# Wider weight operations, two-bank PSUM tiles and five more seven-product pairs in a hybrid encoder block

## The chip, the cores and the metric

The kernel runs on one core of one Trainium2 chip. The metric is the device time of one execution in microseconds (us); lower is better. The engines are named as in the profile: PE is the matrix engine (TensorE) and PEld its weight loads, DVE is VectorE, ACT is ScalarE, POOL is GpSimd, SP issues most of the loads. Work moves between HBM, the on-chip SBUF, and PSUM, the eight banks (128 partitions x 512 floats each) in which matmuls accumulate.

## The reference

One layer over 256 tokens of width 2048, all in float32:

```python
hn = rmsnorm(h, mix_norm_pre)
z, xbc, dt_raw, u = jnp.split(hn @ w_in, ...)             # 2048 x 3616
y_ssd = ssd_mixer(z, xbc, dt_raw, ...)                    # bidirectional Mamba-2 scan, 16 heads of 64
y_pool = pool_mixer(u, pool_w, pool_scale)                # centred mean pooling, 4 windows
h = h + rmsnorm(concat([y_ssd, y_pool]) @ w_out, mix_norm_post)      # 2048 x 2048
hn = rmsnorm(h, ffn_norm_pre)
gate, val = jnp.split(hn @ w_ffn_up, 2, axis=-1)          # 2048 x 11264
ff = (gelu(dwconv(gate, ffn_conv_w, ffn_conv_b)) * val) @ w_ffn_down # 5632 x 2048
h = h + rmsnorm(ff, ffn_norm_post)
gate = sigmoid(rmsnorm(h, ple_norm_pre) @ w_ple_gate)     # 2048 x 2048
h = h + rmsnorm(gate * (p @ w_ple), ple_norm_post)
```

Every weight is used for 256 tokens only, so each is loaded from HBM once, prepared once and used by a few matmuls.

## The kernel before

**Split weights.** The matmuls run on float32r operands. For more precision each float32 weight block is split into a high part (ACT casts it, line 153) and a low part (DVE subtracts the high part from the raw weights, line 154). A product is then three matmuls: high x high, high x low, low x high. The raw weights land in a buffer with tag `raw` (128 x 2048 floats, three of them, line 158); the halves go into tiles with tags `whi` and `wlo` (1056 columns, five of each, lines 149 and 150). One load of 2048 columns, called a unit here, is split as two parts of 1024. A buffer is given again when its last reader has finished, and the tile framework puts in the waits.

**Stages, in order of time.** The first projection `dtu` (dt and the pooling input), three slabs of the conv projection `xbc`, the `z` projection, the output projection `wo`, a small per-layer embedding product `ple`, the up-projection (`ga` and `va`, 176 pieces of 1024 weight columns, line 1010), the down-projection `dn`, and the embedding gate `gt`. `wo`, `dn` and `gt` are done in two halves of 1024 output columns; a half is a loop over pairs of row blocks (`token_major`, line 305). A pair is two 128-row blocks of the weights against two 128-token blocks and two 512-column blocks.

**Pairs by seven products.** A pair is normally 8 block products, 24 matmuls of 512 columns. For pairs listed in `fast`, `dn_fast` and `gt_fast`, `seven_products` (line 255) uses a Strassen-like scheme with 7 products, 21 matmuls. It needs sums of weight blocks (`add_blocks`, line 249: four in-place adds of 512 columns) and sums of activation blocks (`pair_sums`, line 784). For most pairs of `dn` and `gt` the sums of the weight blocks are made during the up-projection (`block_sums`, line 226: fetch, add, store to HBM through POOL's queue) and loaded again as `t`; the pair then loads 1536 raw columns as `r` and 2048 of sums as `t`. Where no sums were made, the pair does its adds in the raw buffer, in place: split part of it, add, split the result. Parts are split as four tiles: `a` (512), `b`, `d`, `c` (1024 each). Activation sums of `dn` are made early for the pairs in `dn_stored`, kept in HBM as `hsum` and fetched as `hd`.

**Order.** In the up-projection ACT, DVE and SP follow the order of the program (`in_order`, line 199); everywhere else the framework's scheduler orders each engine's queue. In the up-projection the parts are split five pieces ahead of their matmuls (line 1008), so the split of part n + 5 waits for piece n. The loads stand on SP's queue in the program's order, each waiting for a free raw buffer; the fetches of the block sums stand between them.

**PSUM.** Two pools: `pmain`, six banks handed out one at a time (`main` takes two), and `pmisc`, two banks. `total` (line 367) adds the two 256-column halves of a bank with one ACT copy and one DVE add per bank.

Of the kernel before, what the change touches and what calls it, by code (L numbers as in the profile page):

```python
# [53 lines left out]
def build(nc, a, out):  # L54
# [6 lines left out]
    with tile.TileContext(nc) as tc, \  # L61
# [6 lines left out]
            tc.tile_pool(name="pmain", bufs=6, space=bass.MemoryType.PSUM) as pm, \  # L68
# [14 lines left out]
        def main(name):  # L83
            return [pm.tile([P, 512], F32, tag="main", name=f"{name}_{i}") for i in range(2)]
# [14 lines left out]
        r0 = wp.tile([P, 2048], F32, tag="raw", bufs=3, name="dtur0")  # L99
# [42 lines left out]
        def split(name, src, nel, cuts=()):  # L142

            if name in ready:
                return ready.pop(name)
            if name in spare:
                hi, lo = spare.pop(name)
            else:
                hi = wp.tile([P, 1056], F32R, tag="whi", bufs=5, name=f"{name}h")
                lo = wp.tile([P, 1056], F32R, tag="wlo", bufs=5, name=f"{name}l")  # L150
            for c0, c1 in zip((0, *cuts), (*cuts, nel)):
                s = slice(c0, c1)
                last["act"] = ins(nc.scalar.copy(hi[:, s], src[:, s]))
                last["dve"] = ins(nc.vector.tensor_sub(lo[:, s], src[:, s], hi[:, s].bitcast(F32)))
            return hi, lo

        def raw(name, src=None):
            r = wp.tile([P, 2048], F32, tag="raw", bufs=3, name=name)
            if src is not None:
                last["dma"] = load(r, src, True)  # L160
            return r

# [86 lines left out]
        def add_blocks(r):  # L249

            v = r.rearrange("p (b c) -> p b c", b=4)
            for i, j in ((1, 0), (0, 3), (3, 1), (2, 3)):
                nc.vector.tensor_add(v[:, i], v[:, i], v[:, j])  # L253

        def seven_products(name, stage, w, k0, c0, a_, acc, alt, start, stop):

            if (stage, c0, k0) in sums_:
                r = raw(f"{name}r")  # L260
                last["dma"] = load(r[:, 512:], w[c0 // 1024, k0 // 2][:, 512:], True)
                t, held = sums_[stage, c0, k0]
                if not held:
                    t = page(f"{name}t")
                    last["dma"] = load(t, sums_[stage, c0, k0][0], True)
            else:
                r = t = raw(f"{name}r", w[c0 // 1024, k0 // 2])
            b11 = split(f"{name}a", r[:, 512:1024], 512)
            b2 = split(f"{name}b", r[:, 1024:], 1024)
            if r is t:  # L270
                add_blocks(r)
            t42 = split(f"{name}d", t[:, 1024:], 1024)
            t31 = split(f"{name}c", t[:, :1024], 1024)

            for x, (wh, wl), c, o, own in (
                    ("a11", b11, 0, alt[0], True), ("a12", b2, 0, acc[0][0], False), ("a22", t42, 0, acc[1][0], False),
                    ("s4", b2, 512, acc[0][1], False), ("s2", t42, 512, alt[3], True), ("s1", t31, 512, alt[1], True),
                    ("s3", t31, 0, alt[2], True)):
                xh, xl = a_[x]
                for q, (xx, ww) in enumerate(((xh, wh), (xh, wl), (xl, wh))):  # L280
                    mm(o, xx, ww[:, c:c + 512], own and start and q == 0, own and stop and q == 2)
# [23 lines left out]
        def token_major(name, w, c0, ks, get, acc, tail=1, fast=(), alt=None, sums=None, at=()):  # L305
# [3 lines left out]
            for u in range(nu):  # L309
# [8 lines left out]
                r = None if f"{name}{k0}_0" in ready else raw(f"{name}r{k0}", w[c0 // 1024, k0 // 2])  # L318
                for j in range(2):
                    group.append((k0 + j, *split(f"{name}{k0}_{j}", r and r[:, j * 1024:(j + 1) * 1024], 1024)))  # L320
# [18 lines left out]
        def feature_major(name, w, get, acc):  # L339

            for u in range(4):
                r = raw(f"{name}r{u}", w[u])
                for j in range(2):
                    wh, wl = split(f"{name}{u}_{j}", r[:, j * 1024:(j + 1) * 1024], 1024)
                    for kk in range(2):
                        k = 4 * u + 2 * j + kk
                        xh, xl = get(k)
                        for f in range(4):
                            s = slice(kk * 512 + f * P, kk * 512 + (f + 1) * P)
                            for q, (ww, xx) in enumerate(((wh, xh), (wh, xl), (wl, xh))):  # L350
                                mm(acc[f // 2][:, f % 2 * L:(f % 2 + 1) * L], ww[:, s], xx,
                                   k == 0 and q == 0 and f % 2 == 0, k == NK - 1 and q == 2)
                aside()

        def feature_pairs(n, part, get, acc):

            wh, wl = part
            for kk in range(4):  # L360
                k = 4 * n + kk
                for f in range(2):
                    s = slice(kk * 256 + f * P, kk * 256 + (f + 1) * P)
                    mm(acc[f], wh[:, s], get.both(k), k == 0, False)
                    mm(acc[f][:, L:], wl[:, s], get(k)[0], False, k == NK - 1)

        def total(o, acc):

            for f in range(2):
                nc.scalar.copy(o[:, f * L:(f + 1) * L], acc[f][:, L:])  # L370
                nc.vector.tensor_add(o[:, f * L:(f + 1) * L], o[:, f * L:(f + 1) * L], acc[f][:, :L])
# [82 lines left out]
        for u in range(0, NK, 2):  # L454
            r = [wp.tile([P, 2048], F32, tag="raw", bufs=3, name=f"dtur{u}") if u else r0, page(f"dtur{u + 1}")]
# [19 lines left out]
            for j in range(2):  # L475
                k = u + j
                with tc.issue_after(front[0]), tc.issue_after(front[1]):
                    wh, wl = split(f"dtu{k}", r[j][:, :1056], 1056, ((352, 704), (704,))[k] if k < 2 else ())
# [305 lines left out]
        def pair_sums(name, s, o, a11, a21, a12, a22):  # L784


            s1, s2, s3, s4 = (s[:, i * P:(i + 1) * P] for i in range(4))
            nc.vector.tensor_sub(s1, a22, a21)
            nc.vector.tensor_sub(s3, a11, a21)
# [6 lines left out]
        def sums_in(o):  # L796
            return {f"s{i + 1}": (o[:, i * P:(i + 1) * P], o[:, 512 + i * P:512 + (i + 1) * P]) for i in range(4)}

        class Sums:
# [5 lines left out]
            def __call__(self, k):  # L805
                if k not in self.got:
                    n = len(self.got)
                    if n % 2 == 0:
# [6 lines left out]
                                            *(v[:, i * P:(i + 1) * P] for i in range(4)))  # L815
# [53 lines left out]
        for t in range(2):  # L869
            load(h[t], x[t * P:(t + 1) * P, :])  # L870
        hf = sublayer("wo", w_out, list(range(8, 16)) + list(range(8)), cat, gload("gmix", a["mix_norm_post"][0]), h,
                      V_FN, Pairs, ((5,), (2, 4)), Sums("cs", cat))
# [26 lines left out]
        for t in range(2):  # L899
# [3 lines left out]
        dn_fast, gt_fast = ((2, 3, 4, 5, 7, 8, 9, 10, 11, 12, 13, 14, 15, 16, 17, 18, 19), (2, 3, 4, 5, 7, 8, 9, 11, 12, 13, 14, 15, 16, 18, 19)), ((4, 5, 6), (1, 2))  # L903

        dn_stored = (2, 3, 5, 7, 8, 10, 11, 13, 14, 16, 17, 18, 19)
        gt_ks = list(range(NK)), [0, 1, 8, 9, 10, 11, 2, 3, 4, 5, 6, 7, 12, 13, 14, 15]
        which = [("dn", w_down, c * 1024, 2 * u) for c in range(2) for u in dn_fast[c]] + \
            [("gt", w_gate, c * 1024, gt_ks[c][2 * u]) for c in range(2) for u in gt_fast[c]]
# [26 lines left out]
        def hid_sums_of(k, s, o):  # L935
            return pair_sums(f"he{k}", s, o, *(hid_part(k)[:, i * P:(i + 1) * P] for i in range(4)))
# [24 lines left out]
        def next_part():  # L961

            n = len(parts)
            if n < NPIECES:
                s, v, i = blocks[n // 4]
                name = f"u{'gv'[v]}{s}{i}"
                if n % 2 == 0:
                    slab["raw"] = raw(f"{name}r{n // 2 % 2}", w_up[v, s, i, n // 2 % 2])
                parts.append(split(f"{name}{n // 2 % 2}_{n % 2}", slab["raw"][:, n % 2 * 1024:(n % 2 + 1) * 1024], 1024))
# [37 lines left out]
        with in_order():  # L1007
            for _ in range(5):
                next_part()
            for n in range(NPIECES):  # L1010
                s, v, i = blocks[n // 4]
                if n % 4 == 0:
                    acc = main(f"{'gv'[v]}a{s}{i}")
# [9 lines left out]
                next_part()  # L1023
# [38 lines left out]
        def ple_parts():  # L1062

            r = raw("ple1r0", w_ple[1, 0])
            for j in range(2):
                ready[f"ple10_{j}"] = split(f"ple10_{j}", r[:, j * 1024:(j + 1) * 1024], 1024)
# [7 lines left out]
        def first():  # L1074

            r, hi, lo = page("gtf"), page("gtfh", F32R), page("gtfl", F32R)
            last["dma"] = load(r, w_gate[0, 0])
            for j in range(2):
                c = slice(j * 1024, (j + 1) * 1024)
                spare[f"gt00_{j}"] = hi[:, c], lo[:, c]  # L1080
                ready[f"gt00_{j}"] = split(f"gt00_{j}", r[:, c], 1024)
# [49 lines left out]
        for half in range(2):  # L1131
# [5 lines left out]
            if half == 1:  # L1137

                for i in (8, 10):
                    sh, sl = page(f"gth{i}", F32R), page(f"gtl{i}", F32R)  # L1140
                    for j in range(2):
                        spare[f"gt1{ks[i]}_{j}"] = (sh[:, j * 1024:(j + 1) * 1024], sl[:, j * 1024:(j + 1) * 1024])
# [99 lines left out]
```

## Time and profile before

| | |
|---|---|
| time, median of three runs | 1116.89 us (1116.58 to 1117.33) |
| span of the profiled execution | 1115.6 us |
| the profiled execution's own time | its span is what the profile gives; the median of the runs is 1.3 us above it |
| PE busy | 1104.8 us, 99% |
| PEld, DVE, ACT, POOL busy | 951.8, 957.5, 721.7, 68.5 us |
| moved by transfers | 347.29 MB, 311 GB/s on average |
| up-projection, about 304 to 788 us | PE without a gap, transfers at 372 GB/s |
| down-projection, about 788 to 1009 us | PE 215.66 of 216 us busy from 790 to 1006 |

How to read it: a page shows one execution. Busy shares are followed by the span in 40 equal slices, each digit the busy tenths of an engine in that slice. The chain of work that ended last is followed back from the last instruction. A timeline row gives start, duration, engine, line, operation, output and inputs; a group row gives count, total busy us and mean ns of one. A waits row says which engine and line waited for which, in total us, times, and the longest. A transfers row gives count, size of one and the median us from issue to landing. The matmuls' ends are modelled, so the pace of PE is read from the distance of starts.

### The profile page before, as it was taken

How to read it: one execution, taken by the hardware profiler on the slowest of the kernel's cores; microseconds unless marked ns; L12 is line 12 of the kernel's file. 1: busy time of each engine (PE TensorE's matmuls, PEld its weight loads, DVE VectorE, ACT ScalarE, POOL GpSimd, SP SyncE). 2: the span in 40 equal slices, each digit the busy share in tenths (PEclk: the TensorE clock that was granted, in tenths of full speed). 3: DMA queues.
4: the chain of work that ended last, by engine and by line, in shares of the span. 5: the costliest groups of instructions: out<-in, count | busy, mean ns of one | idle time of the engine just before them, and what ended most of it. 6: DMA issues, size and time to landing. Idle time of an engine off the chain costs nothing.

```text
span 1115.6 us, 16022 instructions
## 1 busy us (share of the span) xinstructions
PE 1104.8 (99%) x5948; PEld 951.8 (85%) x5948; DVE 957.5 (86%) x1334; ACT 721.7 (65%) x1048; POOL 68.5 (6%) x140
## 2 busy tenths in 40 slices
PE   9999999999999999999999999999999999999997
PEld 9999988888888888888888888888888888877876
DVE  6478997799868898888888888888899999989895
ACT  6847662555775564665655645657589778867673
POOL 0200000100100000000000000000000000001001
PEclk9999999999999999999999999999999999999999
DMA  9752447454599999999899999999999899996763
GB/s 362 314 194 109 164 156 284 151 189 158 199 362 401 387 378 376 359 375 369 346 377 382 354 380 366 353 391 391 361 379 382 329 343 400 418 376 229 264 237 105
DMA packets 54943, 347.29 MB, mean 311 GB/s; under 512 B 6096, under 2 KB 6992, under 8 KB 20176
## 3 DMA queue, kind: packets, MB, share of 16 engines
q1 hardware_dynamic: 44064, 289.53, 67.3%
q0 software_dynamic: 10368, 56.10, 13.4%
q8 instruction: 47, 0.77, 0.3%
q10 hardware_dynamic: 432, 0.62, 0.2%
q14 instruction: 32, 0.26, 0.1%
HBM read 297.48 MB, written 48.76 MB: 310 GB/s over the span
## 4 chain that ended last, share of the span: by engine, by line
PE 94%; DVE 2%; ACT 1%; DMA 1%; issue 1%; POOL 0%; POOLq 0%; ACTq 0%; DVEq 0%
PE ga L90 22%; PE va L90 22%; PE dna L90 12%; PE woa L90 7%; PE xbc L90 5%; PE gt L90 5%; PE z L90 4%; PE dns L90 4%; PE dtu L90 4%; PE dn0s L90 2%; PE dn1s L90 2%; DMA dtur<-w_dtu 1%; PE pw L90 1%; PE yd L90 1%; PE gts L90 1%
## 5 line engine op out<-in xcount | busy, mean ns | idle before, releaser
L90 PE MATMUL ga<-wox,ug_0h 128*128 128x512 f32 x352 | 125.5, 395 | 0.0
L90 PE MATMUL ga<-wox,ug_1h 128*128 128x512 f32 x352 | 125.1, 394 | 0.0
L90 PE MATMUL va<-wox,uv_1h 128*128 128x512 f32 x352 | 124.8, 393 | 0.0
L90 PE MATMUL va<-wox,uv_0h 128*128 128x512 f32 x352 | 124.8, 393 | 0.0
L90 PE MATMUL ga<-wox,ug_1l 128*128 128x256 f32 x352 | 99.1, 282 | 0.0
L90 PE MATMUL va<-wox,uv_1l 128*128 128x256 f32 x352 | 99.1, 281 | 0.0
L90 PE MATMUL va<-wox,uv_0l 128*128 128x256 f32 x352 | 99.1, 281 | 0.0
L90 PE MATMUL ga<-wox,ug_0l 128*128 128x256 f32 x352 | 99.0, 281 | 0.0
L253 DVE TENSOR_TENSOR dnb<-dnb 128x512 f32<-128x512 f32 x128 | 88.3, 690 | 3.1
L90 PEld LDWEIGHTS va<-wox,uv_1h 128*128 128x128 f32 x352 | 66.1, 188 | 15.0
L90 PEld LDWEIGHTS va<-wox,uv_0h 128*128 128x128 f32 x352 | 66.1, 188 | 15.0
L90 PEld LDWEIGHTS ga<-wox,ug_1h 128*128 128x128 f32 x352 | 66.1, 188 | 15.0
L90 PEld LDWEIGHTS ga<-wox,ug_0h 128*128 128x128 f32 x352 | 66.1, 188 | 14.8
L90 PEld LDWEIGHTS ga<-wox,ug_0l 128*128 128x128 f32 x352 | 66.2, 188 | 0.1
L90 PEld LDWEIGHTS ga<-wox,ug_1l 128*128 128x128 f32 x352 | 66.2, 188 | 0.0
L90 PEld LDWEIGHTS va<-wox,uv_1l 128*128 128x128 f32 x352 | 66.2, 188 | 0.0
L90 PEld LDWEIGHTS va<-wox,uv_0l 128*128 128x128 f32 x352 | 66.2, 188 | 0.0
L928 ACT CAST hs<-hid 128x512 fp32r<-128x512 f32 x44 | 27.3, 621 | 21.9 <-PE dna L90 21.6
L244 POOL DMA_DIRECT2D dns<-dnb x30 | 16.3, 542 | 309.4 <-DVE dnb L253 309.4
L929 DVE TENSOR_TENSOR hs<-hid,hs 128x512 fp32r<-128x512 f32 x44 | 30.1, 685 | 5.9 <-ACT hs L928 5.9
L792 ACT CAST he<-he 128x512 fp32r<-128x512 f32 x13 | 8.1, 621 | 36.6 <-DVE he L791 36.6
L90 PE MATMUL dna<-dn_1h,hs 128*128 128x512 f32 x96 | 30.9, 393 | 0.0
(2242 smaller groups left out, 3214.8 us busy)
## 6 DMA issues: line engine op xcount, KB each, us to landing
dnb<-w_down SPq DMA_DIRECT2D x32, 1024.0 KB, 9.9
dns<-dnb POOLq DMA_DIRECT2D x30, 1024.0 KB, 6.9
hd<-hsum POOLq DMA_DIRECT2D x24, 512.0 KB, 8.3
zr<-w_z SPq DMA_DIRECT2D x8, 1024.0 KB, 4.8
dtur<-w_dtu SPq DMA_DIRECT2D x14, 528.0 KB, 8.9
wo0r<-w_out_ SPq DMA_DIRECT2D x7, 1024.0 KB, 4.8
dn1r<-w_down SPq DMA_DIRECT2D x7, 1024.0 KB, 6.6
hsum<-he POOLq DMA_DIRECT2D x13, 512.0 KB, 7.9
```

Source lines behind the costliest of these rows:

```text
L90: last["pe"] = ins(nc.tensor.matmul(o, lhsT, rhs, start=start, stop=stop, skip_group_check=True))
L244: nc.gpsimd.dma_start(t, pg[0])
L253: nc.vector.tensor_add(v[:, i], v[:, i], v[:, j])
L792: nc.scalar.copy(o[:, :512], s[:, :512])
L928: nc.scalar.copy(t[:, :512], hid_part(k))
L929: nc.vector.tensor_sub(t[:, 512:], hid_part(k), t[:, :512].bitcast(F32))
```

## The change

Weight parts are made in one operation of 2048 columns (1536 and 2048 in a pair by seven products) where there were two to four smaller ones. `whi` and `wlo` become three tiles of 2112 columns each in place of five of 1056; the raw buffers become two in place of three. A pair of PSUM banks becomes one tile of 1024 columns, with three tiles in the pool, and `total` handles both banks in one operation per engine. `add_blocks` does its first two adds in one operation with a reversed access pattern; `pair_sums` does two of its subtractions in one.

Five more pairs use seven products, all made in place: pair 6 in the first half of `dn`, pairs 6 and 10 in its second half, pair 5 in the second half of `wo`, pair 3 in the first half of `gt`. In `dn` the in-place pairs use a page instead of a raw buffer. The list of sums made early is the same as before; one more set of activation sums (of pair 6) is stored, and three more are fetched. In the first projection two of the loads that used raw buffers change to other tiles (one is a page).

```diff
-            tc.tile_pool(name="pmain", bufs=6, space=bass.MemoryType.PSUM) as pm, \
+            tc.tile_pool(name="pmain", bufs=3, space=bass.MemoryType.PSUM) as pm, \
...
         def main(name):
-            return [pm.tile([P, 512], F32, tag="main", name=f"{name}_{i}") for i in range(2)]
+            o = both_banks(name)
+            return [o[:, :512], o[:, 512:]]
+
+        def both_banks(name):
+            return pm.tile([P, 1024], F32, tag="main", name=name)
...
-        def split(name, src, nel, cuts=()):
-
-            if name in ready:
-                return ready.pop(name)
-            if name in spare:
-                hi, lo = spare.pop(name)
-            else:
-                hi = wp.tile([P, 1056], F32R, tag="whi", bufs=5, name=f"{name}h")
-                lo = wp.tile([P, 1056], F32R, tag="wlo", bufs=5, name=f"{name}l")
+        def halves(name):
+            return tuple(wp.tile([P, 2112], F32R, tag=f"w{q}", bufs=3, name=f"{name}{q}") for q in ("hi", "lo"))
+
+        def split(hi, lo, src, nel, cuts=()):
+
             for c0, c1 in zip((0, *cuts), (*cuts, nel)):
                 s = slice(c0, c1)
                 last["act"] = ins(nc.scalar.copy(hi[:, s], src[:, s]))
                 last["dve"] = ins(nc.vector.tensor_sub(lo[:, s], src[:, s], hi[:, s].bitcast(F32)))
-            return hi, lo
+            return hi[:, :nel], lo[:, :nel]
 
         def raw(name, src=None):
-            r = wp.tile([P, 2048], F32, tag="raw", bufs=3, name=name)
+            r = wp.tile([P, 2048], F32, tag="raw", bufs=2, name=name)
...
+        def unit(name, src):
+
+            if name in ready:
+                return ready.pop(name)
+            r = raw(f"{name}r", src)
+            return split(*(spare.pop(name) if name in spare else halves(name)), r, 2048)
...
             v = r.rearrange("p (b c) -> p b c", b=4)
-            for i, j in ((1, 0), (0, 3), (3, 1), (2, 3)):
+            nc.vector.tensor_add(v[:, 1::-1], v[:, 1::-1], v[:, ::3])
+            for i, j in ((3, 1), (2, 3)):
                 nc.vector.tensor_add(v[:, i], v[:, i], v[:, j])
...
             else:
-                r = t = raw(f"{name}r", w[c0 // 1024, k0 // 2])
-            b11 = split(f"{name}a", r[:, 512:1024], 512)
-            b2 = split(f"{name}b", r[:, 1024:], 1024)
+                r = t = page(f"{name}r") if stage == "dn" else raw(f"{name}r")
+                last["dma"] = load(r, w[c0 // 1024, k0 // 2], True)
+            bh, bl = split(*halves(f"{name}b"), r[:, 512:], 1536)
             if r is t:
                 add_blocks(r)
-            t42 = split(f"{name}d", t[:, 1024:], 1024)
-            t31 = split(f"{name}c", t[:, :1024], 1024)
+            th, tl = split(*halves(f"{name}t"), t, 2048)
+            b11, b2, t31, t42 = ((h_[:, c0:c1], l_[:, c0:c1]) for h_, l_, c0, c1 in
+                                 ((bh, bl, 0, 512), (bh, bl, 512, 1536), (th, tl, 0, 1024), (th, tl, 1024, 2048)))
...
-            for f in range(2):
-                nc.scalar.copy(o[:, f * L:(f + 1) * L], acc[f][:, L:])
-                nc.vector.tensor_add(o[:, f * L:(f + 1) * L], o[:, f * L:(f + 1) * L], acc[f][:, :L])
+            o, a_ = (v.rearrange("p (f t) -> p f t", f=2) for v in (o, acc))
+            nc.scalar.copy(o, a_[:, :, L:])
+            nc.vector.tensor_add(o, o, a_[:, :, :L])
...
-            r = [wp.tile([P, 2048], F32, tag="raw", bufs=3, name=f"dtur{u}") if u else r0, page(f"dtur{u + 1}")]
+            r = [r0 if u == 0 else page(f"dtur{u}") if u == 4 else raw(f"dtur{u}"), page(f"dtur{u + 1}")]
+            pair = halves(f"dtu{u}")
...
-                      V_FN, Pairs, ((5,), (2, 4)), Sums("cs", cat))
+                      V_FN, Pairs, ((5,), (2, 4, 5)), Sums("cs", cat))
...
-        dn_fast, gt_fast = ((2, 3, 4, 5, 7, 8, 9, 10, 11, 12, 13, 14, 15, 16, 17, 18, 19), (2, 3, 4, 5, 7, 8, 9, 11, 12, 13, 14, 15, 16, 18, 19)), ((4, 5, 6), (1, 2))
-
-        dn_stored = (2, 3, 5, 7, 8, 10, 11, 13, 14, 16, 17, 18, 19)
+        dn_fast, gt_fast = (tuple(range(2, 20)), tuple(u for u in range(2, 20) if u != 17)), ((3, 4, 5, 6), (1, 2))
+
+        dn_stored = (2, 3, 5, 6, 7, 8, 10, 11, 13, 14, 16, 17, 18, 19)
...
+        dn_here, gt_here = ((6,), (6, 10)), ((3,), ())
...
-            for _ in range(5):
-                next_part()
+            for _ in range(3):
+                next_unit()
...
-                next_part()
+                if n % 2:
+                    next_unit()
```

`next_unit` makes the two parts of 1024 columns of an up-projection unit from one call of `unit`; `feature_major` and the plain pairs of `token_major` call `unit` in the same way.

## The prediction on record

> **What bounds the kernel now.** I read the page first (busy shares and slices), then the chain of work that ended last, then the busy time by stage, then durations in the timeline, last the transfers and who waits for them.
>
> ```profile
> span 1115.6 us, 16022 instructions
> PE 1104.8 (99%) x5948; PEld 951.8 (85%) x5948; DVE 957.5 (86%) x1334; ACT 721.7 (65%) x1048; POOL 68.5 (6%) x140
> ...
> PE   9999999999999999999999999999999999999997
> ...
> DVE  6478997799868898888888888888899999989895
> ...
> DMA  9752447454599999999899999999999899996763
> ...
> PE 94%; DVE 2%; ACT 1%; DMA 1%; issue 1%; POOL 0%; POOLq 0%; ACTq 0%; DVEq 0%
> ```
>
> The matrix engine (PE) is busy in all but the last slice, and the chain lies on it for 94%. The chain's pieces in order of time give the price of one matmul:
>
> ```profile
> 142.65 22.18 PE z L90 x96
> ...
> 452.73 22.37 PE va L90 x128
> ...
> 848.68 2.08 PE dna L90 x9
> 853.51 2.07 PE dna L90 x9
> ```
>
> A 512-column matmul takes 22.18 / 96 = 0.231 us. An up-projection value piece of 128 matmuls takes 22.37 us for four weight units of 2048 columns: 5.58 us a unit. Consecutive down-projection pairs by seven products follow each other after 853.51 - 848.68 = 4.83 us, which is 21 x 0.230: PE waits for nothing even there. So PE sets the time everywhere, and any new wait of PE is paid in full. The stages (up, down, z), with DMA share and GB/s last:
>
> ```profile
> core 0: us, PE busy (x) PEld busy (x) DVE busy (x) ACT busy (x) POOL busy (x), PEclk, DMA share, GB/s
> 320.00:787.00 467.00, 467.00 (x2679) 409.94 (x2678) 405.46 (x559) 282.57 (x422) 26.94 (x50) 1.00 0.96 372
> 790.00:1006.00 216.00, 215.66 (x933) 174.23 (x932) 202.94 (x247) 171.28 (x211) 13.17 (x24) 1.00 0.96 372
> 142.00:192.00 50.00, 50.00 (x245) 40.88 (x244) 43.10 (x67) 24.62 (x39) 0.00 (x0) 1.00 0.58 218
> ```
>
> In up and down the transfers are nearly always under way (0.96), and in down VectorE (DVE) has 216 - 203 = 13 us to spare. PE is the bound, with two others close behind.
>
> The profiled span is 1115.6 us; the median of the runs, 1116.89, is 1.3 us more, and I carry that difference unchanged. A difference of 0.2% (2.2 us) is about what can be told from none.
>
> **The change, part by part.**
>
> *Five more pairs by seven products.* Each replaces 24 matmuls by 21; 5 x 3 x 0.231 = 3.5 us less on PE. This is the only part that shortens the path.
>
> *Wider operations.* Durations now, and the price of one block add:
>
> ```profile
> 838.34 0.62 ACT L153 CAST dn022ah<-dn022r 128x512 fp32r<-128x512 f32 x1
> ...
> 838.50 1.22 DVE L154 TENSOR_TENSOR dn020cl<-dn020t,dn020ch 128x1024 fp32r<-128x1024 f32 x1
> ...
> 839.63 0.69 DVE L154 TENSOR_TENSOR dn022al<-dn022r,dn022ah 128x512 fp32r<-128x512 f32 x1
> ...
> 841.11 1.05 ACT L153 CAST dn022dh<-dn022t 128x1024 fp32r<-128x1024 f32 x1
> ```
>
> ```profile
> L253 DVE TENSOR_TENSOR dnb<-dnb x128: 680/691/695, 326.9 to 785.2; 128x512 f32<-128x512 f32 x128
> ```
>
> No row has a 2048-wide split. 512 more columns cost 0.43 us on ScalarE (ACT) and 0.53 on DVE, so I estimate 1.48 and 1.75 us at 1536 columns, 1.90 and 2.29 at 2048. A split of 2048 saves 2 x 1.05 - 1.90 = 0.2 us of ACT and 2 x 1.22 - 2.29 = 0.15 of DVE; the block sums save two adds of 0.69 for one of 1.22, the totals and pair sums some tenths. All this lies on engines that PE hides: worth nothing now, while the latency from arrival to the last low half rises from 1.05 + 1.22 = 2.3 us for the first half unit to 1.90 + 2.29 = 4.2. [...]
>
> *Raw weight buffers, three to two.* This decides. A raw buffer is free when the subtraction has read it, and the load queue (SP) waits for exactly that:
>
> ```profile
> SPq L120 <- DVE ug_1l L154: 162.3, 34, 11.6
> SPq L120 <- DVE uv_1l L154: 131.0, 31, 8.9
> ```
>
> Times from issue to landing (z; first and last of the 40 up rows of two loads each, mean 7.9 us, lowest 6.7; first and last of the 14 rows of the first down half, mean 8.0):
>
> ```profile
> zr<-w_z SPq DMA_DIRECT2D x8, 1024.0 KB, 4.8
> ```
>
> ```profile
> ug10r<-w_up SPq DMA_DIRECT2D x2, 1024.0 KB, 8.0
> ...
> uv101r<-w_up SPq DMA_DIRECT2D x2, 1024.0 KB, 8.0
> ```
>
> ```profile
> hd<-hsum POOLq DMA_DIRECT2D x22, 512.0 KB, 8.3
> ...
> dn010r<-w_down SPq DMA_DIRECT2D x1, 768.0 KB, 7.1
> ...
> dn038r<-w_down SPq DMA_DIRECT2D x1, 768.0 KB, 9.4
> ```
>
> Up: with two buffers, load, cast and subtraction form a loop that serves two units: 7.9 + 1.90 + 2.29 = 12.1 us, against 2 x 5.58 = 11.2 that PE needs. Each round is 0.9 us late. Three buffers have 16.7 us for a loop of that kind, so nothing shows today. Split weights stand two units ahead of PE, which gives 11.2 - 4.2 = 7.0 us of cover once. Over the stage's 44 rounds: 44 x 0.9 - 7 = 33 us if landing stays as it is (upper end); nothing if landing falls under 7.0 us (lower end). Landing shortens when less is asked for: 4.8 us at a share of 0.58, 7.9 at 0.96, by a straight line 8.1 us per unit of share. If the stage stretches by x, the loop is 12.1 - 7.8x and must equal 11.2 (1 + x): x = 0.047, 22 us, less 7 of cover: **15 us**. Between ends so far apart I take this one because both of its points are rows.
>
> Down: the 1536-column loads run through the same two buffers: 8.0 + 1.48 + 1.75 = 11.2 us against 2 x 4.83 = 9.7 for two pairs. Ends: 0, and 17.5 x 1.5 = 26 us for 35 pairs. By the same line, 11.2 - 7.8x = 9.7 (1 + x) gives x = 0.086; of 35 x 4.83 = 169 us that is 14.5, less about 1.6 us of cover in each half: **11 us**. In z and the conv projection landing is 4.8, the loop 9.0, under 11.1: nothing.
>
> [...]
>
> *In place.* Such a pair splits 1536 columns, adds blocks (1.22 + 2 x 0.69, each behind the last) and splits 2048: 1.75 + 2.60 + 2.29 = 6.6 us of DVE, with its activations' split (0.69) 7.3, against 4.83 of PE and 3.1 for the regular unit before. Excess 2.5 us each; ends 0 (DVE's 13 spare us cover it) and 5 x 2.5 = 12.5. In down it partly falls into waits already counted; in the output projection and gate the raw buffer is held through both splits. I take 0.7 each: **3.5 us**. POOL gets one store and three loads of 512 KB more (8.3 us each, prefetched); behind them only later loads of that kind queue.
>
> *Costed at nothing.* The rows these stand on:
>
> ```profile
> L371 DVE TENSOR_TENSOR hid<-hid,va 128x256 f32<-128x256 f32 x44 | 16.6, 415 | 2.6 <-ACT hid L370 2.5
> ...
> L370 ACT COPY hid<-va 128x256 f32<-128x256 f32 x44 | 15.7, 373 | 21.7 <-PE va L90 21.7
> ```
>
> ```profile
> dnb<-w_down SPq DMA_DIRECT2D x32, 1024.0 KB, 9.9
> ```
>
> Weight tiles 5 x 1024 to 3 x 2048: in up a slot frees when PE ends a unit and its split is due two units, 11.2 us, later (4.2 needed). Behind a blocked load SP holds the fetch of a down block, whose add comes three units, 16.7 us, later; its landing is 9.9. PSUM pairs instead of banks: the same six banks, a pair returned when both are read; in up one pair fills for 11.2 us while two more are free, so its evacuation (2 x 0.37 of ACT and 2 x 0.42 of DVE before, overlapping; about 1.2 us) is hidden; without that cover it would cost this at each of 44 blocks. Loads of the first projection move partly to pages, at the same size.
>
> Sum on the profiled span: 1115.6 - 3.5 + 15 + 11 + 3.5 = 1141.6; with 1.3 around it **1143 us**.
>
> **Rivals.**
> 1. Landing does not shorten: 1116.9 - 3.5 + 33 + 26 + 3.5 = 1176 us. For it: loads in the down stage (mean 8.0) are three quarters the size of those in up and land no sooner. Against: z's 4.8.
> 2. Faster. One thing decides, landing: with fewer loads queued at once it falls below 7.0 us in up and 6.4 (9.7 - 1.48 - 1.75) in down, DVE's saved time pays for the adds, and 3.5 us of matmuls go: 1113 us. For it, the two loads of one up block late in the stage (`ug71r`):
>
> ```profile
> DMA to landing us min/median/max: 5.4/6.8/8.2
> ```
>
> Against: the mean of 7.9 while PE never waits, at a share of 0.96.
> 3. Landing in up comes under 7.0 us, as the 5.4 above, in down it does not; only down and the in-place pairs pay: 1116.9 - 3.5 + 11 + 3.5 = 1128 us.
> 4. The loops fit, and the in-place adds give back what the matmuls saved: -3.5 + 3.5, no change, 1117 us.
>
> **How the numbers follow.** Chances: both loops bind with shortened landing 0.40 (1143, own range 1130 to 1158); unchanged landing 0.12; faster 0.22; only down 0.20; no change 0.06. Faster 0.22, same 0.06, slower 0.72. The range runs from the faster case, 1113, to 1165, which leaves out most of the first rival.
>
> **What would show it.** Right: ScalarE waits for loads of up weights (`ACT ..hi <- DMA u..r`) summing to tens of us, PE pieces of 128 matmuls longer than 22.37 us after the first slabs, up longer than 467 us by some 15, pairs in down further apart than 4.83, DMA share below 0.96. Each in-place pair: PE waiting at its `tlo` for DVE. Wrong: landing under 7 us with up still 467 us; then only the -3.5 us and the in-place pairs remain. If PE stalls behind DVE rather than behind loads, the loop was not the cause.

## The result

The changed kernel takes 1212.09 us (median of four runs, 1208.47 to 1214.3) beside 1117.06 us for the kernel before on the same chip: a ratio of 1.0847, 95% interval 1.0827 to 1.0867. It is slower by 95.0 us, where 26 us were predicted; the range ended at 1165.

The page of the changed kernel, the same rows as were shown of before (with the row of the granted clock):

```profile
span 1208.8 us, 15152 instructions
PE 1135.0 (94%) x5933; PEld 960.6 (79%) x5933; DVE 959.5 (79%) x1026; ACT 691.6 (57%) x785; POOL 89.1 (7%) x144
...
PE   9899999997899999999999999999889988999886
...
DVE  6468897787667877878787787788889889889784
...
PEclk9999999998899999999999999999999998999898
DMA  8754456343679999999899989998998799964662
...
DMA 29%; PE 25%; DVE 23%; ACT 15%; issue 7%; POOL 0%; SPq 0%; ACTq 0%; POOLq 0%; DVEq 0%
```

PE now has gaps in most stages. The chain that ended last lay on PE for 94% before; it now runs through DMA, PE, DVE and ACT by turns. There are 15 matmuls fewer, as the five pairs give, yet PE is busy for 30 us longer, and the clock's row has dips that before had not.

Lengths of the stages (from the first matmul on weights of one stage to the first of the next, worked out from the starts of the matmuls in each trace, us) place the loss. The other columns belong to the experiments below. A column is one execution; that of e4 is 5 us under the median of its runs, the others lie within 2 us of theirs.

| stage | before | after | two raw buffers (e1) | five pairs (e3) | after, narrow (e4) | PSUM pairs (e8) | after, three raw (e10) |
|---|---|---|---|---|---|---|---|
| first projection | 48.6 | 52.6 | 50.4 | 48.0 | 52.5 | 49.9 | 50.2 |
| conv projection | 89.1 | 91.0 | 89.0 | 89.2 | 90.2 | 88.8 | 88.9 |
| z | 55.7 | 55.1 | 55.7 | 55.7 | 55.0 | 55.8 | 55.7 |
| output projection | 94.8 | 111.5 | 99.9 | 96.5 | 101.7 | 97.1 | 105.1 |
| up | 494.6 | 514.6 | 554.6 | 501.6 | 514.4 | 495.8 | 502.0 |
| down | 229.2 | 263.4 | 246.8 | 240.5 | 247.4 | 231.3 | 249.6 |
| gate to end | 98.8 | 115.9 | 103.9 | 105.6 | 110.8 | 102.0 | 113.6 |

The loop that the prediction drew is there to be read in the chain of the changed kernel. In down (start, length, what; pieces of a few hundredths left out):

```profile
880.10 1.49 ACT dn018bhi L153
...
881.62 1.77 DVE dn018blo L154
...
883.40 6.92 DMA dn022r<-w_down
...
890.40 1.49 ACT dn022bhi L153
...
891.91 1.77 DVE dn022blo L154
...
893.70 9.35 DMA dn026r<-w_down
...
903.15 1.48 ACT dn026bhi L153
```

Here come a cast, a subtraction, and 0.02 us after it the load of the pair two further on into the same buffer. A round takes 890.40 - 880.10 = 10.3 and 903.15 - 890.40 = 12.75 us, against 2 x 4.83 = 9.66 that PE needs. The durations are the estimated ones (1.48 and 1.75). In up the loop has more in it:

```profile
555.86 7.65 DMA ug511r<-w_up
...
563.61 1.92 ACT ug511hi L153
...
565.55 2.30 DVE ug511lo L154
...
567.87 7.71 DMA uv501r<-w_up
...
575.66 1.91 ACT uv501hi L153
...
579.81 1.23 DVE dnb L259
...
582.48 0.61 DVE gr L379
...
586.72 1.90 ACT uv511hi L153
...
588.65 2.31 DVE uv511lo L154
...
590.97 6.06 DMA ug601r<-w_up
```

The round from the landing at 563.5 over the next load to the cast at 575.66 takes 575.66 - 563.51 = 12.1 us, the forecast figure. From there to the landing at 597.0 the chain goes over block adds, the gate's evacuation and conv, for which the split of `uv511` waits in the ordered queues. But the mean landing time fell too: 6.5 us over the stage (76 rows of one load each, from 330 to 775 us) against 7.9 before. The mean round over the whole stage stands below, at e6 and e7.

### The profile page after: what moved, and what is told of

It reads as the page before. It is cut to its first block, busy times and chain, and to the rows that moved or that the text cites. A ratio compares the mean times of both kernels' runs of the same rounds, so it can differ in the third digit from the quotient of the medians.

```text
span 1208.8 us, 15152 instructions
## 1 busy us (share of the span) xinstructions
PE 1135.0 (94%) x5933; PEld 960.6 (79%) x5933; DVE 959.5 (79%) x1026; ACT 691.6 (57%) x785; POOL 89.1 (7%) x144
## 4 chain that ended last, share of the span: by engine, by line
DMA 29%; PE 25%; DVE 23%; ACT 15%; issue 7%; POOL 0%; SPq 0%; ACTq 0%; POOLq 0%; DVEq 0%
PE xbc L94 6%; PE z L94 4%; PE dna L94 4%; PE woa L94 3%; PE gt L94 2%; DMA dtur<-w_dtu 2%; DVE dnb L261 1%; DMA dn112r<-w_down 1%; DVE dnb L259 1%; DMA x<-x 1%; DMA dn00r<-w_down 1%; DMA dn026r<-w_down 1%; PE dns L94 1%; DMA ug211r<-w_up 1%; DMA dn018r<-w_down 1%
## 5 line engine op out<-in xcount | busy, mean ns | idle before, releaser
L261 DVE TENSOR_TENSOR dnb<-dnb 128x512 f32<-128x512 f32 x64 | 44.3, 692 | 2.1
L259 DVE TENSOR_TENSOR dnb<-dnb 128x1024 f32<-128x1024 f32 x32 | 39.0, 1219 | 0.0
L940 ACT CAST hs<-hid 128x512 fp32r<-128x512 f32 x44 | 27.2, 617 | 11.6 <-PE dna L94 11.5
L998 ACT ACTIVATE fc<-gr,vt 128x256 f32<-128x256 f32 x44 | 26.1, 593 | 10.4 <-DVE gr L991 10.4
L1000 ACT ACTIVATE gr<-gr,vt 128x256 f32<-128x256 f32 x44 | 22.5, 511 | 1.4
L999 ACT ACTIVATE ft<-gr,vt 128x256 f32<-128x256 f32 x44 | 21.8, 495 | 0.0
L447 DVE SCALAR_TENSOR_TENSOR cv<-xr,vt,cv 128x254 f32<-128x254 f32 (+1 forms) x48 | 19.5, 479 | 0.4 <-ACT cv L441 0.3
L1001 DVE TENSOR_TENSOR fc<-fc,ft 128x510 f32<-128x510 f32 x22 | 15.1, 688 | 4.3 <-ACT ft L999 4.0
L1006 ACT ACTIVATE fc<-fc 128x512 f32<-128x512 f32 x22 | 13.8, 628 | 7.3 <-DVE fc L1002 7.3
L1002 DVE TENSOR_TENSOR fc<-fc,gr 128x510 f32<-128x510 f32 x22 | 15.2, 691 | 2.3
L1014 DVE TENSOR_TENSOR hid<-hid,fc 128x512 f32<-128x512 f32 x22 | 15.2, 692 | 0.8
L991 DVE TENSOR_TENSOR gr<-gr,rfb 128x512 f32<-128x512 f32 x22 | 15.2, 692 | 0.8
```

The source lines that it names most:

```text
L259: nc.vector.tensor_add(v[:, 1::-1], v[:, 1::-1], v[:, ::3])
L447: nc.vector.scalar_tensor_tensor(o[:, lo:hi], i[:, lo + d:hi + d], vec(wcol + j * wstep + f), o[:, lo:hi], op0=ALU.mult, op1=ALU.add)
L940: nc.scalar.copy(t[:, :512], hid_part(k))
L998: nc.scalar.activation(c[:, f], v[:, f], AF.Identity, bias=vec(V_FCB + 4 * s + 2 * i + f), scale=vec(w + NF))
L999: nc.scalar.activation(l[:, f], v[:, f], AF.Copy, scale=vec(w))
L1000: nc.scalar.activation(v[:, f], v[:, f], AF.Copy, scale=vec(w + 2 * NF))
```

## The experiments

**Two raw buffers alone (e1).** The kernel before, with one number changed at three places.

```diff
-tag="raw", bufs=3
+tag="raw", bufs=2
```

> The kernel before with two raw weight buffers in place of three, nothing else changed. Theory A (two raw buffers form a loop of load, cast and subtraction that is longer than PE's two units): in up the two half splits stand a piece (2.8 us) apart, so the loop is about 7.9 + 2.8 + 1.05 + 1.22 = 13.0 us against 11.2, up grows by 20 us or more, down by 15 or more, 1155 to 1190 us in all. Theory B (the width of the operations makes the stalls): unchanged, 1115 to 1120. Theory C (the five in-place pairs make them): unchanged, 1115 to 1120.

Measured: 1207.97 us, ratio 1.082 (1.0802 to 1.0838). The number of buffers alone costs what the whole change costs, more than was expected, and most of it in up (+60 us). DVE's rows there:

```profile
471.95 1.22 DVE L154 TENSOR_TENSOR ug_1l<-ug31r,ug_1h 128x1024 fp32r<-128x1024 f32 x1
475.87 1.22 DVE L154 TENSOR_TENSOR ug_0l<-ug31r,ug_0h 128x1024 fp32r<-128x1024 f32 x1
479.66 1.23 DVE L154 TENSOR_TENSOR ug_1l<-ug31r,ug_1h 128x1024 fp32r<-128x1024 f32 x1 [0.26 <-ACT ug_1h L153]
```

With five tiles of 1024 columns the second half of a unit often waits a piece longer for its tile: the two subtractions of the last unit start 3.8 us apart, and the raw buffer is held that long. They start over 3 us apart in 24 of the 67 units loaded from 360 to 770 us. From one load into a buffer to the next, 12.3 us pass on average in e1; with the same narrow splits in tiles for a whole unit (e4, below) it is 11.3, and the changed kernel loses only 20 us in up. So losses of single parts can't be added up here; the wide tiles take back part of what the missing buffer costs.

**The change without the five pairs (e2).** The lists of pairs as before, everything else as after.

```diff
-V_FN, Pairs, ((5,), (2, 4, 5)), ...    dn_fast, gt_fast = (tuple(range(2, 20)), ...   dn_here, gt_here = ((6,), (6, 10)), ((3,), ())
+V_FN, Pairs, ((5,), (2, 4)), ...       dn_fast, gt_fast = ((2, 3, 4, 5, 7, ...        dn_here, gt_here = ((), ()), ((), ())
```

> The changed kernel with the five new pairs taken back (same pairs by seven products as before), wide operations and two raw buffers kept. A: up keeps its 20 us over the kernel before, down some 15 to 25 of its 34; output projection and gate lose a part of their 17 each; 1165 to 1195 us. B: nearly all stays, 1195 to 1212. C: nearly all is gone but up's part, 1130 to 1145.

Measured: 1194.86 us (1187.6 to 1201.8), ratio 1.0695 (1.0638 to 1.0752). The pairs account for some 17 us, with a wide spread; the rest remains without them. The value lies where theories A and B meet, so that it rules out only C. Theory A's share for down did not come: in e2's profile (of its slowest run) down is as long as in the changed kernel, 263.7 us, though three of the five pairs lie there; the gate is 8.8 us shorter and the output projection 2.6.

**Before with the five pairs (e3), and with their adds left out (e5).** Three raw buffers, narrow operations.

```diff
-((5,), (2, 4)) ... dn_fast, gt_fast = ((2, 3, 4, 5, 7, ...
+((5,), (2, 4, 5)) ... dn_fast, gt_fast = (tuple(range(2, 20)), ...
...
             if r is t:                          # e5 alone:
+            if r is t and (stage, c0, k0) not in (("wo", 1024, 2), ("dn", 0, 12), ("dn", 1024, 12), ("dn", 1024, 20), ("gt", 0, 6)):
                 add_blocks(r)
```

> The kernel before (narrow operations, three raw buffers) with the five new pairs in place. A: three buffers hide the loads; 3.5 us of matmuls go and the in-place adds cost up to 3.5 to 8; 1113 to 1122 us. C: the in-place pairs cost what they cost in the changed kernel, 30 us or more; 1145 or more. B: 1113.

> The kernel before with the five new pairs (three raw buffers, narrow operations), as in the run with them at 1143.0 us, but the three block adds in place are left out of these five pairs, so that their operands are wrong and only the time counts. Theory D (the pairs wait for VectorE, which has no time to spare at these places): 5 x 2.7 us of adds go and the stalls with them, 1118 to 1130 us. Rival H (what costs is that a raw buffer is held through both splits, and the loads and stores of the activations' sums): the time stays at 1136 to 1145 us.

Measured: e3 1143.04 us, ratio 1.0231 (1.0215 to 1.0246); e5 1122.42 us, 1.0043 (1.0027 to 1.006). The pairs cost 26 us in a kernel with three raw buffers, where those of down, too, stand in a raw buffer and not in a page; we had expected 1113 to 1122 by our theory. Theory D of e5 is borne out: 20.6 of these us hang on the adds. DVE's timeline at the pair `dn120` in e3, and PE's behind it:

```profile
962.30 0.69 DVE L253 TENSOR_TENSOR dn120r<-dn120r 128x512 f32<-128x512 f32 x1
962.90 1.22 DVE L154 TENSOR_TENSOR gtfl<-gtf,gtfh 128x1024 fp32r<-128x1024 f32 x1
964.04 0.69 DVE L253 TENSOR_TENSOR dn120r<-dn120r 128x512 f32<-128x512 f32 x1
964.64 1.22 DVE L154 TENSOR_TENSOR gtfl<-gtf,gtfh 128x1024 fp32r<-128x1024 f32 x1
965.78 0.69 DVE L253 TENSOR_TENSOR dn120r<-dn120r 128x512 f32<-128x512 f32 x1
966.38 0.69 DVE L930 TENSOR_TENSOR hs<-hid,hs 128x512 fp32r<-128x512 f32 x1
966.98 0.69 DVE L253 TENSOR_TENSOR dn120r<-dn120r 128x512 f32<-128x512 f32 x1
```

```profile
968.86 0.79 PE L90 MATMUL dna<-dn120dh,hs 128*128 128x512 f32 x1 [4.92 <-ACT dn120dh L153]
...
971.13 0.63 PE L90 MATMUL dn1s<-dn120dl,hd 128*128 128x512 f32 x1
971.56 0.63 PE L90 MATMUL dn1s<-dn120dh,hd 128*128 128x512 f32 x1
...
974.93 0.39 PE L90 MATMUL dns<-dn122al,hs 128*128 128x512 f32 x1
975.16 0.39 PE L90 MATMUL dns<-dn122ah,hs 128*128 128x512 f32 x1
```

The four adds depend on one another, and between each two the scheduler has put another operation, so that the chain takes 967.67 - 962.30 = 5.4 us instead of 4 x 0.69 = 2.8; only then may ACT cast the sums. PE has run through what the raw blocks allow and waits 4.92 us. Without the adds, the same wait (profile of e5) is

```profile
PE dna L90 <- ACT dn120dh L153: 0.5, 1, 0.5
```

The rows behind the stall show a second loss: matmuls start 0.43 us apart until 974.5, then 0.23 us again. Its size was measured in e12. This is one of the five pairs, the one with the longest wait; the next section shows that adds strung out like this don't always make PE wait.

**The change with narrow splits (e4).** Same tiles, buffers and pairs; the operations of the splits cut as before.

```diff
-return split(*(spare.pop(name) ... halves(name)), r, 2048)
+return split(*(spare.pop(name) ... halves(name)), r, 2048, (1024,))
...
-bh, bl = split(*halves(f"{name}b"), r[:, 512:], 1536)
+bh, bl = split(*halves(f"{name}b"), r[:, 512:], 1536, (512,))
-th, tl = split(*halves(f"{name}t"), t, 2048)
+th, tl = split(*halves(f"{name}t"), t, 2048, (1024,))
```

> The changed kernel with its buffers, tiles and pairs, but each split of 2048 (or 1536) columns done again as two operations of 1024 (512 and 1024), so that the last low half is ready about 0.8 us sooner. A: the loop in up falls from 12.1 to 11.3 us, just over PE's 11.2; up's 20 us shrink to 5 or less, down's part by a third; 1175 to 1200 us. B: most of the loss is gone, 1120 to 1140. C: nothing changes, 1205 to 1215.

Measured: 1183.71 us, ratio 1.059 (1.0559 to 1.0622). The width of the splits costs 28 us. By the profiles, which are 32 us apart, it is 16 in down, 10 in the output projection, 5 in the gate, and nothing in up as a whole. The time agrees with the theory that named 1175 to 1200, but that up would shrink was wrong. PE's longest waits in down, in the changed kernel and below it in e4, are

```profile
PE dna L94 <- ACT dn120thi L153: 5.0, 1, 5.0
PE dna L94 <- ACT dn112thi L153: 3.1, 1, 3.1
PE dna L94 <- ACT dn012thi L153: 2.5, 1, 2.5
```

```profile
PE dna L94 <- DVE dn010tlo L154: 1.1, 1, 1.1
```

The three waits of the changed kernel are those of the three new pairs in down. All waits of PE for these pairs come to 11.6 us; in e4, with the same pairs and buffers, they come to 2.9 us. It isn't that the adds get through sooner: at `dn012` the three adds run back to back in the changed kernel (2.67 us) and stand among other work in e4 (4.25 us). But one cast of all 2048 columns must wait for the last add and starts at 865.62, 0.9 us after PE began the last of nine matmuls on raw blocks. With the cast in two, ACT casts one half between the adds (at 851.64 in e4), and PE goes on with it and with the next pair. So the wide splits and the pairs in place cost together here.

So in down, output projection and gate the narrower splits let PE go on sooner, by these waits and times; up, at 514.4 against 514.6 us, gains nothing. There two things cancel: in the first 48 us of the stage e4 loses 12.4 us (PE waits 3.2 us at 342.7 for a load that landed late, and the clock is at 0.50 for 6.8 us) and the changed kernel 4.3; over the rest e4 loses 7.3 us and the changed kernel 15.7.

**What binds up (e6, e7).** The changed kernel without the block adds in up, their transfers kept; and without the transfers, the adds kept.

```diff
             def add():                              # e6
-                add_blocks(pg[0])
...
                 pg.append(r)                        # e7
-                load(r, w[c0 // 1024, k // 2])
+                nc.gpsimd.memset(r, 0.0)
...
-                    nc.gpsimd.dma_start(t, pg[0])
-                    sums_[name, c0, k] = t, False
+                    sums_[name, c0, k] = w[c0 // 1024, k // 2], False
```

> The kernel after, with the block adds of the up stage left out (the blocks are still fetched and stored, unsummed, so the pairs that use them get wrong operands). Theory Q (the load, cast and subtraction loop of two raw buffers is stretched by what stands between on VectorE's ordered queue): 32 x 2.6 us of VectorE time go, the up stage falls from 515 us to 498 to 506, the whole to 1192 to 1203 us. Theory T (the loop is bound by the landing time under the traffic): up stays at 511 to 516 us, the whole above 1205 us.

> The kernel after, with the transfers of the block sums left out of the up stage: each page is set to zero by GpSimd instead of fetched, the adds stay, nothing is stored, and the down and gate pairs load the unsummed blocks of the weights in their place (wrong operands, the same traffic there). Theory T (landing under the traffic): landing of up weights falls from 6.5 to about 5.5 us, up falls to 496 to 504 us. Theory Q (ordered work on VectorE): landing falls too, but the adds remain; up stays at 507 to 515 us.

Measured: e6 1214.18 us (ratio 1.0872, 1.0856 to 1.0888), up 513.7; e7 1200.79 us (1.076, 1.071 to 1.081), up 500.1. After the rows above we held the ordered queue of DVE for the cause, theory Q; it falls. The stretch from 360 to 800 us in before, after, e6 and e7 (us; busy PE, PEld, DVE, ACT, POOL; clock, DMA share, GB/s):

```profile
360.00:800.00 440.00, 440.00 (x2506) 385.44 (x2505) 379.68 (x528) 261.01 (x390) 25.07 (x47) 1.00 0.96 372
```

```profile
360.00:800.00 440.00, 429.78 (x2427) 372.29 (x2426) 351.69 (x344) 230.53 (x253) 24.45 (x46) 1.00 0.92 356
```

```profile
360.00:800.00 440.00, 432.85 (x2440) 373.57 (x2439) 270.81 (x244) 231.29 (x255) 24.44 (x46) 1.00 0.93 355
```

```profile
360.00:800.00 440.00, 440.00 (x2540) 384.97 (x2539) 369.74 (x362) 246.36 (x274) 58.55 (x43) 1.00 0.58 207
```

Without the adds DVE has 81 us less to do, but the loads land later (mean 7.1 us instead of 6.5) and up stays as long. Without the block transfers the share is 0.58, landing 4.9 us on average, nearly z's 4.8 at the same share, and PE has no gap left. The mean round of a raw buffer, worked out from the starts of loads, casts and subtractions of the units loaded from 360 to 770 us, shows why (us):

| | landing | until the cast | cast | until the subtraction | subtraction | until the next load | round |
|---|---|---|---|---|---|---|---|
| after | 6.52 | 0.33 | 1.91 | 0.46 | 2.29 | 0.03 | 11.54 |
| without block adds (e6) | 7.04 | 0.22 | 1.91 | 0.04 | 2.29 | 0.03 | 11.53 |
| without block transfers (e7) | 4.91 | 1.57 | 1.91 | 0.40 | 2.29 | 0.03 | 11.11 |

PE needs 2 x 5.58 = 11.16 us for the two units of a round. In e7 the loads land early and the cast waits, mostly for work that follows PE, so the round is PE's own. In the other two it is 0.4 us longer, about 17 us over the 44 rounds, which is most of the 20 lost in up. So up is bound by the loop through landing times under the block sums' traffic. What DVE saves in e6 (0.5 us a round), landing takes back. E7 also takes the fetches out of the load queue, but the next load follows the subtraction by 0.03 us with and without them, so the queue isn't what costs.

**Small wide operations (e8, e9).** Before with the three-add block sums, the three-operation pair sums, PSUM in three pairs and totals over a pair (e8); the same without the PSUM pairs and their totals (e9).

```diff
-tc.tile_pool(name="pmain", bufs=6, ...      # e8 alone, with total() over a pair
+tc.tile_pool(name="pmain", bufs=3, ...
...
-for i, j in ((1, 0), (0, 3), (3, 1), (2, 3)):
+nc.vector.tensor_add(v[:, 1::-1], v[:, 1::-1], v[:, ::3])
+for i, j in ((3, 1), (2, 3)):
```

> The kernel before with the wide operations that touch no weight buffer: block sums by three adds instead of four, pair sums by three operations instead of four, the up blocks' totals by one copy and one add over a PSUM pair, and PSUM in three pairs instead of six banks. Three raw buffers and half-width splits stay. As predicted (all of it beside PE): 1112 to 1118 us. Rival P (PSUM pairs come free later than single banks and stall PE at the 44 blocks): 44 x up to 1.2 us, 1120 to 1170 us.

> The kernel before with only the block sums by three adds and the pair sums by three operations; the accumulators stay six single banks and the totals go bank by bank as before. In the run with all small wide operations and PSUM in pairs the time was 1127.8 us, 10.7 more than before, spread over the ends of the stages. Theory P (the pairs of PSUM banks are what costs: two halves come free only together): 1114 to 1118 us. Rival S (the wider small operations cost, by holding VectorE longer at one time): 1122 to 1130 us.

Measured: e8 1127.77 us, ratio 1.0096 (1.0081 to 1.0111); e9 1117.34 us, 1.0002 (0.9992 to 1.0012). The merged sums are worth nothing, as predicted; PSUM in pairs, with the totals over a pair, costs 10.4 us. It isn't paid at the 44 blocks of up (up +1.2), but spread over where stages meet or end. PE's longest wait in e8, at the last product of the kernel, and below it the same wait before:

```profile
PE gof L94 <- ACT godg L1124: 4.3, 1, 4.3
```

```profile
PE gof L90 <- ACT godg L1117: 1.9, 1, 1.9
```

That the halves coming free together is the reason was argued, not shown.

**The change with three raw buffers (e10).** Room comes from the low halves: two tiles instead of three, and up splits two units ahead instead of three.

```diff
-tag="raw", bufs=2 ... tag=f"w{q}", bufs=3 ... for _ in range(3): next_unit()
+tag="raw", bufs=3 ... tag=f"w{q}", bufs=3 if q == "hi" else 2 ... for _ in range(2): next_unit()
```

> The kernel after with three raw buffers; to make room, the low halves of split weights have two tiles instead of three (the high halves keep three), and the up stage splits two units ahead instead of three. Theory R (the two raw buffers are what lengthens the up stage): up falls from 514.6 to 495 to 503 us. Rival W (the width of the split with the ordered work around it): up stays at 510 us or more. In the down stage a pair needs both low tiles at once, so its time there says nothing on the raw buffers alone; the whole is 1150 to 1215 us by R, 1195 to 1240 by W.

Measured: 1170.59 us, ratio 1.048 (1.0464 to 1.0496), up 502.0 us. From 360 to 800 us PE has no gap, although loads now land later (mean 8.2 us):

```profile
360.00:800.00 440.00, 440.00 (x2499) 382.48 (x2498) 365.89 (x359) 241.05 (x274) 26.14 (x49) 1.00 0.96 367
```

The third buffer, less what the missing low tile may cost, gives 41.5 us back. Of the remaining 7.4 us of up, 3.1 lie in its first 50 us. The rest builds up evenly and without waits, as a 512- and a 256-column matmul together take 0.352 us instead of 0.349; why is open. In e3 the 7.0 us lost in up all lie in its first matmuls.

**What a stall of PE costs (e11, e12).** Before, with three waits put into z.

```diff
+def stall():
+    o, w = misc("stallp"), sp.tile([P, 512], F32, tag="junk", bufs=1, name="stall")
+    mm(o[:, :P], ident, ident, True, True); nc.scalar.copy(w[:, :P], o[:, :P])    # e12 alone
+    for _ in range(8):
+        nc.gpsimd.memset(w, 0.0)
+    mm(o[:, :P], w[:, :P], ident, True, True)       # e12: the next matmuls of z are put behind it
...
+token_major("z", ..., at={u: stall for u in (2, 4, 6)})
```

> The kernel before with three stalls put into the z stage, 11 us of matmuls apart: PE waits each time for eight writes of a 128x512 tile by GpSimd, some 4 to 5 us, and then for nothing. If a stall costs what it lasts: z grows by the sum of the three waits, 12 to 15 us. Theory C (the granted clock falls behind a stall, as the matmuls of 0.427 us behind the 5.09 us stall in the run with five pairs): z grows by 2 to 4 us more per stall, 18 to 27 us in all.

> As the run with three stalls, in which PE did not wait because GpSimd wrote its tile long ahead. Now each round of eight writes (4.6 us in that run) starts from a copy by ScalarE of what a matmul of PE left, and the next matmuls of z are put behind it, so that PE has nothing to do for about 5 to 5.5 us, three times in or at the end of z. If a stall costs what it lasts: 1132 to 1134 us (three times 5 to 5.5 us, less some 1 us of other matmuls that fall into it). Theory C (the granted clock falls behind a stall): 2 to 4 us more per stall, 1138 to 1146 us.

Measured: e11 1118.3 us, ratio 1.0011 (1.0002 to 1.0021), and no wait in the trace: GpSimd wrote its tile far ahead and the scheduler moved the matmul, so this run tells nothing of stalls. e12: 1139.32 us beside 1117.25, ratio 1.0193 (1.0176 to 1.021). PE's gaps in it, the first in three pieces, are 4.4, 5.9 and 3.9 us, 14.1 us together; the time grew by 22.1. The second stall and two stretches of 5 us around it (columns as above):

```profile
178.95 0.79 PE L91 MATMUL stallp<-ident,stall 128*128 128x128 f32 x2 [5.73 <-POOL stall L750]
```

```profile
175.00:180.00 5.00, 1.05 (x4) 0.95 (x5) 0.34 (x1) 0.00 (x0) 3.55 (x7) 0.84 0.46 187
180.00:185.00 5.00, 5.00 (x13) 3.94 (x12) 0.00 (x0) 0.10 (x1) 0.00 (x0) 0.50 0.02 3
185.00:190.00 5.00, 5.00 (x23) 4.00 (x22) 2.26 (x2) 2.00 (x2) 0.00 (x0) 0.98 0.33 95
```

In the 5 us behind the stall the granted clock is 0.50: 13 matmuls in place of 23. The starts of the slow matmuls behind the three stalls, taken against 0.231 us each, give 7.7 us, and 14.1 + 7.7 = 21.8 of the 22.1 us. Theory C holds.

## Why the prediction was wrong

*What bounds the kernel:* right, PE set the time everywhere. But "any new wait of PE is paid in full" is too little: by e12 three stalls of 14.1 us cost 22.1. In the changed kernel the record of the granted clock shows ten stretches at 0.50, 47.8 us together, ahead of the last product of the kernel. They cost at most half of that, 24 of the 95 us. In the kernel before there is none while PE works.

*Five pairs, -3.5 us:* 5933 matmuls instead of 5948, but the gain is nowhere to be seen. Even without their adds the pairs cost 5.4 us (e5); that this is because DVE, at 203 of 216 us in down, has no room for what else they bring is argued.

*Wider operations, worth nothing:* right for the merged sums (e9). Wrong for the splits: 28 us (e4). The prediction had the longer latency, 4.2 us instead of 2.3, but set it against the 11.2 us of cover in up alone. In down it had the wide durations in the loop of the buffers, but nowhere, in the output projection, down or gate, did it price that a pair must wait for a whole split of 1536 or 2048 columns.

*Raw buffers:* near in up and down, too small as a whole (26 us taken, 41.5 by e10). After against e10, the loop costs 514.6 - 502.0 = 12.6 us in up (taken: 15) and 263.4 - 249.6 = 13.8 in down (taken: 11); z loses nothing, as said. Missing were the output projection (6.4), the first two projections (2.4 + 2.1, the second of which was put at nothing) and the gate (2.3); part of e10's difference may come from its two low tiles. Landing did shorten, but not by the straight line: at a share of 0.92 the line gives 4.8 + 8.1 x 0.34 = 7.6 us, the trace 6.5. And the loop was not only load, cast and subtraction: the round of 11.54 us has 0.8 us of waits in it, for which the sum had no term. That the round came out near the forecast 11.2 x 1.047 = 11.7 us is luck: two errors of opposite sign. Alone, in the kernel before, the same step costs 91 us (e1).

*In place, 0.7 us a pair:* this failed most. The term was 3.5 us (ends 0 and 12.5); e3 shows 26 us, and e2 some 17 within the change, for pairs that should also have saved 3.5. The step added up DVE's time, 6.6 us against 4.83, and set its excess against 13 us of slack in the whole stage. What counts is the chain of one pair: adds that depend on one another in a queue which other work shares, then the cast, all of it after the last add where it is one operation, then PE, and a clock of 0.50 behind it (e3). The forecast "PE waiting at its `tlo` for DVE" was out by one step: PE waits for the high half, which ACT casts once DVE has added (`dn120thi`, 5.0 us, above).

*PSUM pairs, at nothing:* wrong by 10.4 us (e8 against e9), though not at the blocks for which the prediction named a price.

What the runs give for the parts: the third raw buffer 41.5 us (after against e10), the five pairs 26 alone (e3) and 17 within the change (e2), the wide splits 28 within the change (e4), the PSUM pairs 10.4 alone. They overlap, as e1 and e4 show, so they don't add up to a proof; 41.5, 26 and 10.4 leave 17 of the 95 us, which no run shows separately. So the sum failed in three terms: the pairs in place at 3.5 us, the wider operations at nothing and the PSUM pairs at nothing.

The forecast's likeliest case and the first rival had the right sign and, for the loop, the right mechanism. Landing came as the third rival supposed, under 7.0 us in up (6.5 on average) and not under 6.4 in down (6.7 and 7.1 in its halves); but that up would then lose nothing was wrong: 6.5 + 1.90 + 2.29 = 10.7 us would fit into 11.2, and with the 0.8 us of waits the round is 11.5.

No version here beats the kernel before; e9 equals it.

## What to carry to other kernels

Where loads, casts and subtractions refill a buffer, work out the loop for each stage, with all that stands between on ordered queues, before giving up a buffer; its largest term here, landing, was 6.5 us under the block sums' traffic and 4.9 without it (e7). A dependent chain on a busy engine is priced by when its last link is done and by how much of the next operation must wait for that link, not by its busy time against the stage's slack: in e3 four adds of 0.69 us took 5.4, and PE waited 4.92. A stall of PE cost more than it lasted where the clock fell behind it: 1.6 times as much in e12.

## What was not expected of the hardware

The granted clock was 0.50 in the 5 us behind the stall of 4.92 us in e3, and behind the one of 5.9 us in e12. It didn't take 5 us: in up of the changed kernel the clock fell with a wait of 2.35 us (PE's timeline; before and after the wait, pairs of a 512- and a 256-column matmul):

```profile
699.49 0.40 PE L94 MATMUL ga<-wox,ug801hi 128*128 128x512 f32 x1
...
699.85 0.40 PE L94 MATMUL ga<-wox,ug801hi 128*128 128x512 f32 x1
...
702.95 0.41 PE L94 MATMUL ga<-wox,ug810lo 128*128 128x256 f32 x1 [2.35 <-DVE ug810lo L154]
703.17 0.61 PE L94 MATMUL ga<-wox,ug810hi 128*128 128x512 f32 x1
...
703.79 0.63 PE L94 MATMUL ga<-wox,ug810hi 128*128 128x512 f32 x1
```

A pair of matmuls takes 699.85 - 699.49 = 0.36 us ahead of the wait and 703.79 - 703.17 = 0.62 behind it; the mean clock is 1.00 from 695 to 700 us and 0.82 and 0.84 in the next two stretches of 5 us.

The length of the wait alone did not decide. In down of the same run PE waits 2.47 us for `dn012thi`, until 867.57, and the clock stays at 1.00 from 865 to 880 us; from 867.90 on, matmuls that wait for nothing start 0.23 or 0.24 us after the one before. So a wait of about the same length can cost more or less; what decides was not shown.

With less work on DVE the loads landed later: without the block adds (e6), landing rose from 6.5 to 7.1 us at the same rate (356 and 355 GB/s), and the stage was as long as with them. Why landing takes up just what the other steps leave is not shown.
